# Pinned means, later constants and a GpSimd split at the hand-over from projection to attention

## The chip, the cores and the metric

The kernel runs on one core of a Trainium2 chip. The metric is the device time of one execution in microseconds. A core has five engines with a queue of instructions each: TensorE (PE; its weight loads are listed as PEld), VectorE (DVE), ScalarE (ACT), GpSimd (POOL) and SyncE (SP, which here only issues transfers). Each engine works through its own queue in order; an instruction that has to wait holds up everything behind it on that engine. POOL and SP both issue the transfers of the paged cache.

## The reference, cut to what matters

One decoder layer is computed for a prompt of 1024 tokens and for a sample group of 8 sequences with 8 new tokens each, whose 4096 past tokens lie in a paged cache (256 pages of 128 tokens). Both groups share the weights.

```python
h = rms_norm(x, norm1) * (1 + scale1) + shift1
z = h @ w_in
q, kc, vc, ks, vs, kw, vw, gates, conv..., pool_in = split(z)
q  = rms_norm(q, q_gain)                     # per head of 64 channels
ks = rms_norm(ks, k_gain[1]); kw = rms_norm(kw, k_gain[2])
k_cmp = rms_norm(compress(kc of past and new), k_gain[0]); v_cmp = compress(vc ...)
o_cmp, p_cmp = attention(q, k_cmp, v_cmp)    # compressed blocks
top_i = top_k(block importance from p_cmp)   # selected blocks
o_slc = attention(q, selected blocks of ks, vs)
o_win = attention(q, last 512 of kw, vw)
o = g0 * o_cmp + g1 * o_slc + g2 * o_win     # sigmoid gates
x = x + gate1 * (concat[o, conv(z), pool(z)] @ w_out)
x = x + gate2 * swiglu(rms_norm(x, norm2) * (1 + scale2) + shift2)
```

Every large product is done in three matmuls of a high and a low half (`hi*hi + lo*hi + hi*lo`), so each fp32 operand is first split: ACT writes the rounded high half, and DVE or POOL subtracts it from the value to get the low half (`split`, whose low half is L171 and whose high half is L175).

## The kernel before, in words

The 1088 tokens (1024 of the prompt, 64 of the samples) lie along the free axis in three chunks of 384, 384 and 320. The stages are: the conditioning and the norm; the input projection; attention for prompt and samples together; the output projection; the feed-forward part. PSUM is dealt out anew between stages (`psum_phase`): during the projection six banks hold accumulators, during attention six hold scores and two hold accumulations.

**Input projection.** Sixteen weight tiles of 128 output columns are each multiplied with the three chunks. `project` (L708) issues 24 matmuls for a chunk (eight slices of the contraction, three products each). The last four tiles are the query's, q0 to q3. For these, and for ks and kw, a coroutine `head_norm` (L752) is spawned per chunk: Square on ACT (L757), a matmul with the matrix `mean_h` on PE which forms the mean over each head's channels, the square root on ACT (L762), the reciprocal on DVE (L765), and the scaling on DVE (L766). The scaling reads the chunk's accumulator, and so sets that PSUM bank free.

**The hand-over.** `attention` (L1458) writes the masks (POOL and DVE), splits two stacks of keys (`key_stacks`, L1042: K[0] for the selected and compressed branches, K[1] for the window; each 1024 columns from the projection and 64 compressed ones), splits the first query columns (`query_parts`, L1064), writes constants that only the samples need (`constants3`, L282), and copies the sample queries and keys (`sample_setup`, L1220). The last two are issued after the last scaling of the projection (`issue_after`).

**Attention.** 32 prompt units (`prompt_attention`) alternate between branch slc and branch win: score matmuls into six PSUM banks, an evacuation on DVE with mask and minimum (L1123), exponent on ACT (L1135), two small operations by the gate on DVE (L1137 to L1141), a multiply on POOL (L1145), transposes on PE (L143) and value matmuls. Between them run the samples. Their cache is compressed in octets: eight pages of 128 KB are loaded into one of three `stream` buffers, six by SP and two by POOL (L520 to L538), and PE multiplies them in 16 matmuls, each of which is two records of the trace. The first three of the eight sequences are compressed before the hand-over. `sample_select` (L1236) then chooses blocks for a pair of sequences, after loading that pair's compressed keys (`kvc`, L1247); it runs four times. `sample_attention` reads the pages again in units of 16 (`unit`).

**What sets the order.** Stages are Python generators. A planner (`run`, L85) keeps an estimated clock for each engine. Of the tasks whose due time has come it steps the one of lowest priority number; `use` adds an estimated cost to an engine and `hold` waits for a condition. This gives the order in which instructions are written; a scheduler behind it then orders each engine's queue by its own simulation, bounded by `high_priority` and `issue_after`.

Of the kernel before, what the change touches and what calls it, by code (L numbers as in the profile page):

```python
# [17 lines left out]
P = 128  # L18
# [26 lines left out]
PACE = 0.5  # L45
EPS = 1e-6
# [16 lines left out]
class Kernel:  # L63
# [218 lines left out]
    def constants3(self, c):  # L282
        nc = self.nc
        with self.pool("ctmp") as tp:

            ti = tp.tile([P, 1], I32, name="ti")
            nc.gpsimd.iota(ti, pattern=[[0, 1]], base=0, channel_multiplier=1)
            t7 = tp.tile([P, 1], I32, name="t7")
            nc.vector.tensor_scalar(t7, ti, 7, None, op0=OP.bitwise_and)
            tv = tp.tile([P, 1], F32, name="tv")  # L290
            nc.vector.tensor_copy(tv, t7)


            di = tp.tile([P, P], I32, name="di")
            nc.gpsimd.iota(di, pattern=[[1, P]], base=P, channel_multiplier=-1)
            d7 = tp.tile([P, P], I32, name="d7")
            nc.vector.tensor_scalar(d7, di, 7, None, op0=OP.bitwise_and)
            eq = tp.tile([P, P], F32, name="eq")
            nc.vector.tensor_scalar(eq, d7, 0.0, None, op0=OP.is_equal)
            self.rsum = c.tile([P, P], F32, name="rsum")  # L300
            nc.gpsimd.memset(self.rsum, 0.0)
            for q in range(4):
                s = slice(32 * q, 32 * q + 32)
                nc.vector.tensor_copy(self.rsum[s, s], eq[s, s])


            a = tp.tile([P, 4, 64], F32, name="a")
            for b2 in range(2):
                nc.gpsimd.iota(a[64 * b2:64 * b2 + 64], pattern=[[-16, 4], [1, 64]], base=-8 * b2,
                               channel_multiplier=0, allow_small_or_imprecise_dtypes=True)  # L310
            ge = tp.tile([P, 4, 64], F32, name="ge")
            nc.vector.tensor_scalar(ge, a, 0.0, None, op0=OP.is_ge)
            ok = tp.tile([P, 4, 64], F32, name="ok")
            nc.vector.scalar_tensor_tensor(ok, a, tv[:, 0:1], ge, op0=OP.is_le, op1=OP.mult)
            self.m_new = c.tile([P, 4, 64], F32, name="m_new")
            nc.vector.tensor_scalar(self.m_new, ok, -1.0, 1e30, op0=OP.add, op1=OP.mult)


            w = tp.tile([P, 8], F32, name="w")
            nc.gpsimd.iota(w, pattern=[[1, 8]], base=0, channel_multiplier=0, allow_small_or_imprecise_dtypes=True)  # L320
            self.m_win = c.tile([P, 512], BF16, name="m_win")
            nc.gpsimd.memset(self.m_win, 0.0)
            nc.vector.tensor_scalar(self.m_win[:, 0:8], w, tv[:, 0:1], NEG, op0=OP.is_le, op1=OP.mult)


            self.sel = c.tile([P, 4, P], F32, name="sel")
            si = tp.tile([P, 4, 2, 8, 8], F32, name="si")
            for p in range(4):
                nc.gpsimd.iota(si[:, p], pattern=[[-8, 2], [0, 8], [-1, 8]], base=-64 - 16 * p,
                               channel_multiplier=1, allow_small_or_imprecise_dtypes=True)  # L330
            nc.vector.tensor_scalar(self.sel.rearrange("a p r -> a (p r)"), si.rearrange("a p b g t -> a (p b g t)"),
                                    0.0, None, op0=OP.is_equal)


            hi = tp.tile([P, 8], F32, name="hi")
            for b2 in range(2):
                nc.gpsimd.iota(hi[64 * b2:64 * b2 + 64], pattern=[[-8, 8]], base=0, channel_multiplier=1,
# [2037 lines left out]
```

## Time and profile before

| | us |
|---|---|
| median of three runs | 1656.8 (1656.56 to 1657.72) |
| the profiled execution's own time | 1654.03 |
| its span | 1652.4 |
| PE busy | 1565.2 (95%) |
| DVE busy | 1092.2 (66%) |
| ACT busy | 775.7 (47%) |
| POOL busy | 656.3 (40%) |
| mean granted clock of PE | 0.981 |

The span is what the profiler's records cover. The projection ends at about 368 us of it, attention lies between 368 and 817, and the output projection and the feed-forward part follow. A row of a timeline gives the start, the duration, the engine, the line, the operation with its tiles, and how many instructions were taken together; a bracket gives the idle time of the engine ahead of it and the instruction that ended it. The granted clock is the share of full speed at which PE was let run.

### The profile page before, as it was taken

The page shows a single profiled execution, that of the slowest core. Times are in us where ns is not written, and L with a number is a line of the kernel's source. Part 1 is how long each engine was busy: PE and PEld are TensorE (multiplying, and loading weights), DVE is VectorE, ACT ScalarE, POOL GpSimd, SP SyncE. Part 2 cuts the span into 40 slices and gives each one's busy share as a digit, 9 for nine tenths or more (in the row PEclk, how much of TensorE's full clock was granted, in tenths as well). Part 3 has the DMA queues.
Part 4 walks back from the last instruction along what each step waited for, and adds up shares of the span by engine and source line. Part 5 has one row for each costly group of instructions (what it writes and reads, how often), then busy time and mean ns, then how long its engine had stood idle before and what let it go on. Part 6 is the DMA issues. An engine that isn't in the chain of part 4 may idle for free.

```text
span 1652.4 us, 35479 instructions
## 1 busy us (share of the span) xinstructions
PE 1565.2 (95%) x12569; PEld 1388.2 (84%) x12569; DVE 1092.2 (66%) x2645; ACT 775.7 (47%) x1828; POOL 656.3 (40%) x789
## 2 busy tenths in 40 slices
PE   6999999997999899899999989999999999899998
PEld 2899997895777666566699989999999999899998
DVE  4713224876555666767589878777777775577668
ACT  3522215434765667656576534343434333344444
POOL 3111110213333133222213356554544554788765
PEclk9999999998999899999999999999999999999999
DMA  9576665425467373244696565336443335967643
GB/s 339 188 266 188 193 182 169 147 77 163 136 179 219 108 211 97 78 132 126 194 319 213 189 224 185 139 137 232 147 146 138 138 136 199 380 244 249 217 159 125
DMA packets 194659, 302.12 MB, mean 183 GB/s; under 512 B 25841, under 2 KB 131634, under 8 KB 194162
## 3 DMA queue, kind: packets, MB, share of 16 engines
q1 hardware_dynamic: 175346, 272.17, 49.5%
q0 software_dynamic: 6208, 17.38, 3.3%
q10 hardware_dynamic: 12928, 10.29, 2.1%
q8 instruction: 100, 1.64, 0.4%
q14 instruction: 77, 0.63, 0.1%
HBM read 233.43 MB, written 70.53 MB: 184 GB/s over the span
## 4 chain that ended last, share of the span: by engine, by line
PE 74%; DVE 11%; ACT 5%; DMA 4%; issue 3%; POOL 2%; SPq 0%; ACTq 0%; DVEq 0%; POOLq 0%
PE bank L139 70%; PE bank L143 4%; DVE P L1123 2%; ACT P L1135 2%; DVE w_lo L171 1%; DMA w_raw<-in_wup 1%; DMA w_raw<-in_wout 1%; ACT w_hi L175 1%; DMA x<-x_d 1%; POOL P L1145 1%; POOL b_t L171 1%; DMA x<-in_xT 1%; DVE h_lo L474 1%; DVE b_lo L171 0%; DVE ml L171 0%
## 5 line engine op out<-in xcount | busy, mean ns | idle before, releaser
L139 PE MATMUL bank<-b_hi,w_hi 128*128 128x272 f32 x1232 | 351.3, 290 | 7.0 <-DVE pair L1722 2.9
L139 PE MATMUL bank<-b_lo,w_hi 128*128 128x272 f32 x1232 | 353.5, 289 | 1.7 <-DVE b_lo L171 1.7
L139 PE MATMUL bank<-b_hi,w_lo 128*128 128x272 f32 x1232 | 348.8, 288 | 1.3 <-DVE w_lo L171 0.9
L139 PEld LDWEIGHTS bank<-b_hi,w_hi 128*128 128x128 f32 x1232 | 230.5, 189 | 10.4 <-ACT b_hi L175 4.0
L139 PEld LDWEIGHTS bank<-b_lo,w_hi 128*128 128x128 f32 x1232 | 232.4, 189 | 2.4 <-DVE b_lo L171 2.3
L139 PEld LDWEIGHTS bank<-b_hi,w_lo 128*128 128x128 f32 x1232 | 230.6, 189 | 1.8 <-DVE w_lo L171 1.1
L1145 POOL TENSOR_SCALAR P<-P,st 128x128 f32<-128x128 f32 (+10 forms) x192 | 109.1, 582 | 232.7 <-DVE st L1141 141.3
L171 DVE TENSOR_TENSOR w_lo<-w_raw,w_hi 128x512 fp32r<-128x512 f32 (+2 forms) x120 | 114.6, 965 | 81.8 <-ACT w_hi L175 81.6
L171 POOL TENSOR_TENSOR w_s<-w_raw 128x512 f32<-128x512 f32 (+1 forms) x88 | 124.3, 1412 | 70.3 <-DVE w_lo L171 53.4
L175 ACT ACTIVATE w_hi<-w_raw 128x512 fp32r<-128x512 f32 (+2 forms) x122 | 80.6, 677 | 132.5 <-PE bank L139 87.7
L139 PEld LDWEIGHTS bank<-stream 128*128 128x128 f32 x1056 | 128.8, 200 | 16.0 <-issue 11.9
L139 PE MATMUL bank<-stream 128*128 128x128 f32 x1056 | 135.1, 286 | 1.8 <-DMA stream<-in_cacheA 1.1
L1135 ACT ACTIVATE P<-P,st 128x128 f32<-128x128 f32 (+12 forms) x192 | 112.7, 588 | 45.8 <-DVE st L1129 28.6
L171 POOL TENSOR_TENSOR x<-x,d_m 128x272 f32<-128x272 f32 x136 | 118.0, 887 | 34.2 <-DVE x L1925 17.5
L139 PE MATMUL bank<-h_hi,w_hi 128*128 128x384 f32 (+1 forms) x384 | 129.4, 337 | 0.4 <-DVE q L766 0.4
L139 PE MATMUL bank<-h_hi,w_lo 128*128 128x384 f32 (+1 forms) x384 | 126.6, 330 | 0.0
L139 PE MATMUL bank<-h_lo,w_hi 128*128 128x384 f32 (+1 forms) x384 | 126.4, 329 | 0.0
L171 DVE TENSOR_TENSOR w_lo<-w_s,w_hi 128x512 fp32r<-128x512 f32 (+1 forms) x124 | 115.7, 935 | 15.9 <-ACT w_hi L175 13.7
L139 PE MATMUL bank<-g,w_hi 128*128 128x272 f32 x616 | 121.4, 293 | 4.7 <-DVE x L1925 4.7
L139 PE MATMUL bank<-g,d_hi 128*128 128x272 f32 x616 | 119.1, 289 | 2.3 <-DVE x L1928 1.6
L1925 DVE SCALAR_TENSOR_TENSOR x<-bank,mod,x 128x272 f32<-128x272 f32 (+1 forms) x200 | 90.2, 476 | 39.1 <-PE bank L139 28.2
L175 ACT ACTIVATE w_hi<-w_s 128x512 fp32r<-128x512 f32 (+1 forms) x124 | 76.6, 621 | 64.5 <-PE bank L139 35.4
(376 smaller groups left out, 3756.3 us busy)
## 6 DMA issues: line engine op xcount, KB each, us to landing
g<-g_d SPq DMA_DIRECT2D x63, 544.0 KB, 6.1
g_d<-f_s SPq DMA_DIRECT2D x57, 544.0 KB, 3.4
wada<-in_wada SPq DMA_DIRECT2D x96, 256.0 KB, 5.3
stream<-in_cacheA SPq DMA_DIRECT2D x192, 128.0 KB, 3.2
w_raw<-in_wup SPq DMA_DIRECT2D x40, 512.0 KB, 4.3
unit<-in_cacheB SPq DMA_DIRECT2D x152, 128.0 KB, 2.4
stream<-in_cacheB SPq DMA_DIRECT2D x104, 128.0 KB, 2.2
w_raw<-in_wout SPq DMA_DIRECT2D x24, 512.0 KB, 5.7
```

Source lines behind the costliest of these rows:

```text
L139: return self.nc.tensor.matmul(out, lhsT, rhs, start=start, stop=stop, skip_group_check=chain)
L143: return self.nc.tensor.transpose(out, in_, self.ident if ident is None else ident)
L171: (self.nc.vector if eng == "dve" else self.nc.gpsimd).tensor_tensor(out, a, b, op=op)
L175: self.last_hi = self.nc.scalar.activation(hi, src, AF.Copy)
L474: nc.vector.scalar_tensor_tensor(lk, t, sh[:, k, 0:1], hk.bitcast(F32), op0=OP.add, op1=OP.subtract)
L1123: nc.vector.tensor_tensor_reduce(out=Pt[:, 2 * g + hl, col:col + n], in0=S[g][:, p0:p0 + n], in1=mk, scale=-1.0, scalar=3e38, op0=OP.add, ...
L1135: nc.scalar.activation(Ps, Ps, AF.Exp, scale=-1.0, bias=sy[:, g, 0:1], accum_out=sy[:, g, 1:2])
L1145: nc.gpsimd.tensor_scalar(Ps, Ps, sy[:, g, 3:4], 0.0, op0=OP.mult, op1=OP.add)
L1925: self.last_gate = nc.vector.scalar_tensor_tensor(out[:, :n], acc[:, :n], self.mod[:, 5, m, 0:1], out[:, :n], op0=OP.mult, op1=OP.add)
```

## The change

The change has four parts.

1. The last query tile, q3, is `PINNED`: of each chunk only four of the eight contraction slices are written, then the planner steps other tasks until the preceding `head_norm` has written its instructions, and the other four slices are issued after that head's mean matmul.
2. In `attention`, `query_parts` comes ahead of `key_stacks`. `constants3` leaves its place ahead of `sample_setup` and is issued after the last softmax evacuation of the first prompt unit. Its scratch tiles now live in the pool of the attention stage, not in a pool of their own. The samples' attention is held until the constants are written.
3. In `key_stacks`, the low halves of the second stack (window) are computed on GpSimd.
4. `sample_select` for a pair is held until the selection of the pair before is over (`selected`).

```diff
+PINNED = ("q3",)
...
     def constants3(self, c):
         nc = self.nc
-        with self.pool("ctmp") as tp:
-
-            ti = tp.tile([P, 1], I32, name="ti")
...
+        tp = c
+
+
+        ti = tp.tile([P, 1], I32, name="ti")
...
-    def project(self, w, h, ch, n):
-        acc = self.bank()
-        for k in range(KT):
+    def project(self, w, h, ch, n, acc=None, ks=range(KT)):
+        acc = self.bank() if acc is None else acc
+        for k in ks:
             self.mm3(acc[:, :n], (w[0][:, k], w[1][:, k]), (h[ch][0][:, k, :n], h[ch][1][:, k, :n]),
                      k == 0, k == KT - 1)
         return acc[:, :n]
...
-            self.mm(m[:, :n], self.mean_h, sq[:, :n], True, True)
+            self.last_mean = self.mm(m[:, :n], self.mean_h, sq[:, :n], True, True)
...
-                        acc = self.project(w, h, ch, n)
+                        if nm in PINNED:
+                            heads = self.heads
+                            acc = self.project(w, h, ch, n, None, range(KT // 2))
+                            yield from self.hold(lambda: self.heads > heads)
+                            with self.tc.issue_after(self.last_mean.ins):
+                                self.project(w, h, ch, n, acc, range(KT // 2, KT))
+                        else:
+                            acc = self.project(w, h, ch, n)
                         step(nm, ch, acc, c0, n)
...
         for j in range(2):
             kh, kl = self.K[j]
             for a, n, src in ((64, SEQ, self.ksw[:, j, 0:SEQ]), (0, 64, self.kcp)):
-                self.split(kh[:, a:a + n], kl[:, a:a + n], src, n)
+                self.stacks_at = self.split(kh[:, a:a + n], kl[:, a:a + n], src, n, eng="pool" if j else "dve")
                 yield max(self.t["dve"], self.t["act"]) - 1.0
-        self.stacks_at = max(self.t["dve"], self.t["act"])
...
+            if u == 0 and hl == 1:
+                self.first_evac = self.last_evac
+                self.scored = True
             yield 0.0
...
-        yield from self.hold(lambda: self.cmp_done >= 2 * p + 2)
+        yield from self.hold(lambda: self.cmp_done >= 2 * p + 2 and self.selected == p)
...
+        self.selected += 1
...
     def attention(self, ap, kp_, opened):
         self.masks(ap)
         self.use("dve", 1.0)
+        self.query_parts(ap, 0)
         yield from self.key_stacks()
-        self.query_parts(ap, 0)
         with self.tc.issue_after(self.last_scale.ins):
-            self.constants3(ap)
             self.sample_setup(ap)
-        self.use("dve", 5.0)
         kp_.__exit__(None, None, None)
         pp = opened.enter_context(self.pool("prompt"))
         self.spawn(lambda: 1.8 + self.v_done / 32, self.prompt_attention(pp))
+        yield from self.hold(lambda: self.scored)
+        with self.tc.issue_after(self.first_evac.ins):
+            self.constants3(ap)
+        self.use("dve", 3.2)
+        self.constants_done = True
 
     def sample(self, opened, cp, batches):
         share = lambda: 1.9 + 0.4 * (self.cmp_done - EARLY) / (NB - EARLY)
         self.spawn(share, self.compress(cp, batches, 0))
         sp = opened.enter_context(self.pool("samp", "left"))
+        yield from self.hold(lambda: self.constants_done)
         yield self.t["dve"]
```

How this moves the instructions is seen in the engines' queues. First PE, at the end of the input projection, before; `h_hi_107` and `h_lo_108` are the halves of the third chunk, `h_sq,mean_h` is a head's mean (128x384 of the second chunk, 128x320 of the third):

```order
L139 MATMUL bank<-h_hi_107,w_hi 128x320
L139 MATMUL bank<-h_lo_108,w_hi 128x320
L139 MATMUL bank<-h_hi_107,w_lo 128x320
L139 MATMUL bank<-h_sq,mean_h 128x384
L139 MATMUL bank<-h_sq,mean_h 128x320
L139 MATMUL bank<-stream 128x128 x16
```

And the same place now; the line numbers of the changed file are higher by one here:

```order
L140 MATMUL bank<-h_hi_107,w_hi 128x320
L140 MATMUL bank<-h_lo_108,w_hi 128x320
L140 MATMUL bank<-h_hi_107,w_lo 128x320
L140 MATMUL bank<-h_sq,mean_h 128x384
L140 MATMUL bank<-h_hi_107,w_hi 128x320
L140 MATMUL bank<-h_lo_108,w_hi 128x320
L140 MATMUL bank<-h_hi_107,w_lo 128x320
```

The second chunk's mean stood behind all 24 matmuls of the third chunk; now it stands behind twelve of them, and the other twelve follow it. The third chunk's mean (128x320) is still the last matmul ahead of the octet. PE executes the same matmuls, only the order is another.

Second, DVE at the hand-over, before; `kl_3450` is the low half of the first key stack and `kl_3452` that of the second, `ql` the query's, and L264 to L273 write the masks:

```order
L171 TENSOR_TENSOR kl_3450<-kv__98,kh_3449 128x1024
L171 TENSOR_TENSOR kl_3450<-kcp,kh_3449 128x64
L264 CAST m_slc<-m 128x128
L264 CAST m_edge<-m 128x128
L264 CAST m_cmp<-m 128x8
L171 TENSOR_TENSOR kl_3452<-kv__98,kh_3451 128x1024
L171 TENSOR_TENSOR kl_3452<-kcp,kh_3451 128x64
L273 COPY m_edge<-m_slc 128x128
L171 TENSOR_TENSOR ql<-q,qh 128x512 x2
L765 RECIPROCAL h_sq<-h_sq 128x384
L765 RECIPROCAL h_sq<-h_sq 128x320
L766 SCALAR_TENSOR_TENSOR q<-bank,qgain_s,h_sq 128x384
```

And now:

```order
L767 RECIPROCAL h_sq<-h_sq 128x384
L172 TENSOR_TENSOR ql<-q,qh 128x512
L768 SCALAR_TENSOR_TENSOR q<-bank,qgain_s,h_sq 128x384
L172 TENSOR_TENSOR kl_3450<-kv__98,kh_3449 128x1024
L265 CAST m_slc<-m 128x128
L172 TENSOR_TENSOR kl_3450<-kcp,kh_3449 128x64
L265 CAST m_edge<-m 128x128
L265 CAST m_cmp<-m 128x8
L172 TENSOR_TENSOR ql<-q,qh 128x512
L274 COPY m_edge<-m_slc 128x128
L767 RECIPROCAL h_sq<-h_sq 128x320
L768 SCALAR_TENSOR_TENSOR q<-bank,qgain_s,h_sq 128x320
```

The second chunk's reciprocal and scaling moved ahead of the first stack's low half, and the second stack's low half is gone from DVE. Behind these rows stood, before, the last scaling, the operations of `constants3` mixed with those of `sample_setup` and the first selection's memsets, and then the first evacuation; now only the setup and the memsets stand there. On POOL the two subtractions of `kl_3452` stand behind the last `iota` of the constants and ahead of the two cache pages (`stream`) that POOL issues.

Third, SP's queue where it comes to the second selection's compressed keys (`kvc`); `stream` are pages of octets. Before:

```order
L530 ISA
L530 DMA stream<-in_cacheA 128x256
L1247 DMA kvc<-cmp_d 128x512
L526 TENSOR_LOAD pt
L530 ISA
L530 DMA stream<-in_cacheA 128x256
```

And now:

```order
L532 ISA
L532 DMA stream<-in_cacheA 128x256
L1258 DMA kvc<-cmp_d 128x512 x2
L528 TENSOR_LOAD pt
L532 ISA
L532 DMA stream<-in_cacheA 128x256
```

From the hand-over on SP's queue held, before, the first selection's two `kvc` loads, 6 stream loads (one octet), 16 unit loads, 18 stream loads, one `kvc` load, 10 stream loads and the other `kvc` load. Now it holds the first two `kvc` loads, 18 stream loads (three octets), the same 16 unit loads, 30 stream loads, and then two `kvc` loads together: the unit loads stand behind two more octets, and the second selection's loads behind 48 stream loads where the first of them stood behind 24.

More of the change, by code (lines that the diff above doesn't have):

```diff
@@ L283, in constants3 @@
         nc = self.nc
-        with self.pool("ctmp") as tp:
-            ti = tp.tile([P, 1], I32, name="ti")
[L287 to L337, printed above, removed]
-                               allow_small_or_imprecise_dtypes=True)
-            hg = tp.tile([P, 8], F32, name="hg")
-            nc.vector.tensor_scalar(hg, hi, 0.0, None, op0=OP.is_ge)
-            self.hind = c.tile([P, 8], F32, name="hind")
-            nc.vector.scalar_tensor_tensor(self.hind, hi, 7.0, hg, op0=OP.is_le, op1=OP.mult)
@@ new lines, in constants3 @@
+        nc.vector.tensor_scalar(d7, di, 7, None, op0=OP.bitwise_and)
+        eq = tp.tile([P, P], F32, name="eq")
+        nc.vector.tensor_scalar(eq, d7, 0.0, None, op0=OP.is_equal)
+        self.rsum = c.tile([P, P], F32, name="rsum")
+        nc.gpsimd.memset(self.rsum, 0.0)
+        for q in range(4):
+            s = slice(32 * q, 32 * q + 32)
+            nc.vector.tensor_copy(self.rsum[s, s], eq[s, s])
+        a = tp.tile([P, 4, 64], F32, name="a")
+        for b2 in range(2):
+            nc.gpsimd.iota(a[64 * b2:64 * b2 + 64], pattern=[[-16, 4], [1, 64]], base=-8 * b2,
+                           channel_multiplier=0, allow_small_or_imprecise_dtypes=True)
@@ new lines, in constants3 @@
+        self.m_win = c.tile([P, 512], BF16, name="m_win")
+        nc.gpsimd.memset(self.m_win, 0.0)
+        nc.vector.tensor_scalar(self.m_win[:, 0:8], w, tv[:, 0:1], NEG, op0=OP.is_le, op1=OP.mult)
+        self.sel = c.tile([P, 4, P], F32, name="sel")
+        si = tp.tile([P, 4, 2, 8, 8], F32, name="si")
+        for p in range(4):
+            nc.gpsimd.iota(si[:, p], pattern=[[-8, 2], [0, 8], [-1, 8]], base=-64 - 16 * p,
+                           channel_multiplier=1, allow_small_or_imprecise_dtypes=True)
@@ new lines, in constants3 @@
+        nc.vector.tensor_scalar(self.sel.rearrange("a p r -> a (p r)"), si.rearrange("a p b g t -> a (p b g t)"),
+                                0.0, None, op0=OP.is_equal)
+        hi = tp.tile([P, 8], F32, name="hi")
+        for b2 in range(2):
+            nc.gpsimd.iota(hi[64 * b2:64 * b2 + 64], pattern=[[-8, 8]], base=0, channel_multiplier=1,
+                           allow_small_or_imprecise_dtypes=True)
+        hg = tp.tile([P, 8], F32, name="hg")
+        nc.vector.tensor_scalar(hg, hi, 0.0, None, op0=OP.is_ge)
@@ L2186, in build @@
         self.combined = 0
+        self.scored = self.constants_done = False
         self.n2_done = 0
@@ L2221, in build @@
         self.post_free = True
+        self.selected = 0
         self.constants2()
```

20 lines of the change are left out of this document (19 added, 1 removed).

## The prediction

> **What bounds the kernel now.** I read the page first, then TensorE's waits, the row of every engine around its longest wait, and last the same stretches as windows. The page's first part:
>
> ```profile
> PE 1565.2 (95%) x12569; PEld 1388.2 (84%) x12569; DVE 1092.2 (66%) x2645; ACT 775.7 (47%) x1828; POOL 656.3 (40%) x789
> ```
>
> PE is busy for 95% of the span, so another engine matters only where it makes PE stop. The waits of PE from 378 to 800 us (us in all, times, the longest):
>
> ```profile
> PE bank L143 <- POOL P L1145: 12.1, 6, 3.2
> PE bank L139 <- DVE q L766: 6.6, 1, 6.6
> PE bank L139 <- DVE st L1123: 5.0, 5, 2.7
> PE bank L139 <- DMA stream<-in_cacheA: 1.1, 1, 1.1
> ```
>
> One wait of 6.6 us stands alone: the hand-over from the input projection to attention. PE's rows there (start, duration, then what it does; in brackets the idle time before it and its releaser):
>
> ```profile
> 363.33 0.32 PE L139 MATMUL bank<-h_hi,w_hi 128*128 128x320 f32 x1
> ...
> 366.86 1.50 PE L139 MATMUL bank<-h_sq,mean_h 128*128 128x384 f32 x4
> 368.19 3.73 PE L139 MATMUL bank<-stream 128*128 128x128 f32 x32
> 378.50 0.89 PE L139 MATMUL bank<-kh,qh 64*128 64x192 f32 x2 [6.58 <-DVE q L766]
> ...
> 380.06 0.36 PE L139 MATMUL bank<-kh,qh 64*128 64x128 f32 x1
> 383.18 0.44 PE L139 MATMUL bank<-kh,qh 64*128 64x128 f32 x1 [2.71 <-DVE st L1123]
> ...
> 384.61 8.53 PE L139 MATMUL bank<-stream 128*128 128x128 f32 x64
> 393.07 1.00 PE L143 MATMUL bank<-ident,P 64*128 64x64 f32 x12
> ```
>
> The last means end the projection, one octet of the cache (x32) fills PE to 371.92, then PE stands for 6.58 us until the heads' scaling on DVE, computes the first scores, and stands 2.71 us more for the softmax evacuation (L1123): 9.3 us idle. DVE has no gap there:
>
> ```profile
> 363.97 2.56 DVE L765 RECIPROCAL h_sq<-h_sq 128x384 f32<-128x384 f32 x1 [2.81 <-ACT h_sq L762]
> ...
> 368.47 1.23 DVE L171 TENSOR_TENSOR kl<-kv__98,kh 128x1024 fp32r<-128x1024 f32 x1 [1.30 <-ACT kh L175]
> ...
> 370.86 1.16 DVE L171 TENSOR_TENSOR kl<-kv__98,kh 128x1024 fp32r<-128x1024 f32 x1
> ...
> 372.17 1.28 DVE L171 TENSOR_TENSOR ql<-q,qh 128x512 fp32r<-128x512 f32 x2
> 373.37 4.55 DVE L765 RECIPROCAL h_sq<-h_sq 128x384 f32<-128x384 f32 x2
> 377.85 0.97 DVE L766 SCALAR_TENSOR_TENSOR q<-bank,qgain_s,h_sq 128x384 f32<-128x384 f32 x2
> 378.74 0.14 DVE L289 TENSOR_SCALAR t<-ti 128x1 int32<-128x1 int32 x1
> ...
> 379.67 0.48 DVE L1223 MEMSET qb<- 128x512 f32 x1
> ...
> 380.55 0.57 DVE L1226 COPY qb<-q 64x256 f32<-64x256 f32 x2
> ...
> 382.65 0.28 DVE L1123 CUSTOM_DVE_ANT_0 P<-bank,m_slc 128x128 f32<-128x128 f32 x1
> ```
>
> In order: both stacks' low halves (kl), the query's (ql), two reciprocals (2.56, the second 4.55 - 2.56 = 2.0), two scalings, then 3.9 us of constants and sample setup before the first evacuation at 382.65. The first scores sit behind both scalings, since these empty the PSUM banks that the scores take. The windows (us; busy time of PE, PEld, DVE, ACT, POOL; granted clock; DMA share; GB/s):
>
> ```profile
> 371.90:378.50 6.60, 0.03 (x1) 0.03 (x1) 6.60 (x9) 0.00 (x0) 3.75 (x14) 0.87 0.67 200
> 384.60:387.00 2.40, 2.40 (x12) 2.39 (x12) 1.12 (x10) 2.40 (x17) 0.56 (x2) 0.50 0.64 201
> 387.00:393.00 6.00, 6.00 (x55) 5.95 (x54) 1.69 (x8) 1.62 (x9) 4.45 (x13) 1.00 0.36 103
> 392.00:396.00 4.00, 4.00 (x38) 2.93 (x38) 2.08 (x13) 2.72 (x11) 1.08 (x2) 1.00 0.92 282
> 414.40:421.00 6.60, 6.51 (x34) 5.48 (x35) 3.09 (x26) 4.73 (x22) 2.95 (x8) 0.50 0.00 0
> 817.00:1652.40 835.40, 807.23 (x6321) 798.50 (x6321) 631.08 (x1141) 374.59 (x840) 458.22 (x444) 0.99 0.57 197
> ```
>
> The idle time has a second price: until 387.0 the granted clock is 0.50, and an octet's matmul then takes 2.40/12 = 0.20 us, against 3.73/32 = 0.117 in the first octet. Each us of octets at half clock thus loses 1 - 0.117/0.20 = 0.41 us. From 817 on PE is busy for 807.23 of 835.40 us in an order that the change keeps, so what is gained before stays.
>
> **The change part by part.**
>
> *Pinned means.* No matmul is added. The mean of q3's second chunk stood behind the 24 matmuls of the third; now it follows the twelfth. These 24 take 366.86 - 363.33 = 3.53 us, 0.147 each, so the mean starts 1.8 us earlier, at 365.1, and ends (half of 1.50) at 365.85. ACT's square roots are
>
> ```profile
> 370.62 0.98 ACT L762 ACTIVATE h_sq<-bank,eps 128x384 f32<-128x384 f32 x2
> 383.01 1.28 ACT L1135 ACT_TABLE_LOAD   x1 [11.41 <-issue]
> ```
>
> 0.49 each, and this one no longer stands behind the splits: done at 366.4. DVE then has reciprocal 2.56 (369.0), one ql 0.64, scaling 0.49: 370.2, before the octet ends. The third chunk's mean stays last.
>
> *Low halves and query parts.* The first stack's kl (1.23) still precedes the scores: 371.4, so they start about when the octet ends, at 371.92, and the 6.58 us wait goes. Its short piece and the casts take the rest of the 370.86 - 368.47 = 2.39 us between the two kl rows: 372.6; the second ql 0.64: 373.2. The second stack's kl (372.17 - 370.86 = 1.3 with its short piece) leaves DVE. **Late next** is the third chunk's scaling: reciprocal 2.0, scaling 0.49: 375.7. The window scores need its bank.
>
> *Constants.* Of the 3.9 us from 378.74 to 382.65, the setup from 379.67 to 381.12 (380.55 + 0.57) stays, without the five constants' operations between its own some 1.4 us; 2.5 us leave the path. The displaced constants run between later evacuations, under PE's octets (DVE is busy for 1.69 of 387.0 to 393.0); uncovered, they would cost that 2.5. The evacuation starts at 375.7 + 1.4 = 377.1. The table load (1.28), which stood at 383.01 although ACT had been idle for 11.41 us, moves ahead of it; nothing in the sum counts on that.
>
> *The planner's holds and due times* (`selected`, `constants_done`, `stacks_at`, 3.2 for 5.0) issue nothing; they act through the order alone, which is the first and the third rival.
>
> *GpSimd.* The page's group for the same kind of operation, and POOL's rows:
>
> ```profile
> L171 POOL TENSOR_TENSOR w_s<-w_raw 128x512 f32<-128x512 f32 (+1 forms) x88 | 124.3, 1412 | 70.3 <-DVE w_lo L171 53.4
> 370.81 1.24 POOL L279 TENSOR_SCALAR_AFFINE_SELECT rowok<-rowok 128x1 f32<-128x1 f32 x1
> ...
> 374.42 0.33 POOL L337 IOTA hi<- 64x8 f32 x2
> 375.80 1.17 POOL L530 DMA_DIRECT2D stream<-in_cacheA  x2 [1.06 <-issue]
> 386.44 3.88 POOL L1145 TENSOR_SCALAR P<-P,st 128x128 f32<-128x128 f32 x12 [9.46 <-ACT P L1135]
> ```
>
> 1.41 us for 512 columns is 2.8 for 1024 (an estimate); behind the iotas (374.75) it ends near 377.6. Only the window scores' second matmuls want it, and these stand behind the evacuation's first half us, so it is hidden, with nothing to spare: each us that POOL starts later would be PE's. Two things are queued behind it: two octet pages, whose issue slips from 375.80 to 378.9 (allow 0.3 us, bounds 0 and 0.9), and the multiplies by st, which start far later and end 2.7 us (393.07 - 386.44 - 3.88) before the transposes take them. DVE may suffer too: rowok, one column wide, took 1.24 us just while DVE's two-input kl ran (370.86 to 372.02). Turned round, kl on POOL may hold DVE's setup copies until it ends: bounds 0 and 1.4 us. The Trainium skill, page "SBUF — State Buffer", section "SBUF: two separate sides", speaks against this part of the change: VectorE and GpSimd share one port pair as an exclusive lock, and the loser waits out a whole instruction. The rowok row agrees; by this rule the sum below would lie at its upper end, 1.4 us later.
>
> *The sum.* The following octet started 384.61 - 382.65 = 1.96 us behind the first evacuation. It would now start at 379.1, or 380.5 with the whole lock: 5.5 or 4.1 us earlier; I take the middle, 4.8. Against that: the clock that stayed at 0.50 for 2.4 us of octets will, with the octets reached sooner after an idle stretch, perhaps stay for 3.4: 0.4 us. It could be 0 (a gain of 2.4 x 0.41 = 1.0) or 5 us (a loss of 1.1). The pages cost 0.3. Net 4.8 - 0.4 - 0.3 = 4.1 us; ends 5.5 + 1.0 = 6.5 and 4.1 - 1.1 - 0.9 = 2.1. The profiled execution took 1654.03 us (span 1652.4), 2.8 below the runs' median of 1656.8; the saving is the same in both: 1649.9 on the profiled one, **1652.7 us** on the median. The Trainium skill, page "TensorE: Matmul & The Clock Gate", section "Part 1: The HAM clock gate", has the clock follow a window of some 3.4 us, so that gaps of 2.5 us would not halve it. By it the sum would take the 1.0 gain; 414.40 to 421.00, at 0.50 with PE busy for 6.51 of 6.60 us, disagrees at least on how soon it returns.
>
> **Rivals.**
>
> *The order behind wins more.* The change also moves the octets and the paged loads (`selected == p` holds the second selection back until the first is over):
>
> ```profile
> 416.31 6.12 PE L139 MATMUL bank<-stream 128*128 128x128 f32 x32
> 422.46 1.37 SPq L530 DMA_DIRECT2D stream<-in_cacheA  x3
> ```
>
> This octet runs at half clock behind short waits, SP's next page can only start when it has freed its buffer, at 422.46, and from 414.40 to 421.00 nothing is transferred. With octets closer together one could lie among those short waits. Worth: 6.5 x 0.41 = 2.7 of clock and some 1.0 of waits just ahead of it (an estimate: the POOL P row of the waits gives 12.1 in 6, and half of one such is taken), on top of 4.1: 7.8, so 1649.0. Against it: waits of that length can form elsewhere in the new order.
>
> *The clock eats it.* Both octets at half clock throughout: 64 x 0.20 = 12.8 in place of 8.53, 4.3 lost of 4.8, 0.3 for the pages: gain 0.2, 1656.6. For it speaks the clock at 387.0, which came back only 8.5 us after PE did; against it, that the gaps shrink.
>
> *Slower: octets starve.* Octets now stand closer together, and 16 unit loads have been moved behind those of two more octets:
>
> ```profile
> 375.51 9.82 SPq L530 DMA_DIRECT2D unit<-in_cacheB  x16
> 475.06 1.58 PE L139 MATMUL bank<-stream 128*128 128x128 f32 x12 [1.14 <-DMA stream<-in_cacheA]
> ```
>
> An octet is 1 MB: 3.7 us at the 282 GB/s of 392 to 396, exactly the 3.73 that PE spends on it. Back to back, nothing is spare. From the point where three octets stand with less than 3.7 us of other work between, each waits; at the 475.06 row's 1.1 us for nine of them, +9.9 - 4.1: 1662.6. Against it: that wait occurred once in 440 us.
>
> *It doesn't do what it says* would be the mean still waiting in ACT's queue; the Square of the third chunk cannot start before the chunk ends, so the square root precedes it. I give this nothing of its own.
>
> **How the numbers follow.** Forecast 0.50 (own range 1650.3 to 1654.7), order 0.16 (1649.0), clock 0.16 (1656.6), starving 0.18 (1662.6). A measurement here tells 0.2%, 3.3 us, from no change. The forecast's 4.1 is beyond that in three quarters of its range: 0.37 faster, 0.13 same. So faster 0.37 + 0.16 = 0.53, same 0.13 + 0.16 = 0.29, slower 0.18. The range reaches from below the order's case, 1646, into the starving one, 1661 (its milder half); about 0.05 and 0.1 stay outside.
>
> **What would show it.** Right: no wait for q at L766 near 372; a wait of about 2.5 us for the third chunk's scaling or the evacuation; the octet pair at 379 to 380 instead of 384.61; kl on POOL at 2.5 to 2.8 us. The lock: DVE copies of over 1 us beside it. Clock: the octet pair longer than 9 us. Starving: PE waits for stream in the list of waits, over 3 us in all. The forecast falls if PE reaches 817's work less than 3 us or more than 7 us earlier than before.

## The result, and the profile after

The changed kernel takes 1673.3 us (median of six runs, 1668.49 to 1679.92) against 1657.2 us before (also the median of six): the ratio is 1.0101, with a 95% interval of 1.0072 to 1.013. The forecast was 1652.7 us, faster, with a range to 1661. The sign was wrong, and the time lies outside the range.

The profiled execution took 1668.49 us, with a span of 1666.9. PE's rows at the hand-over, in the changed kernel (start, duration, what; in brackets the idle time before and its releaser):

```profile
359.85 0.31 PE L140 MATMUL bank<-h_hi,w_hi 128*128 128x320 f32 x1
...
364.70 0.81 PE L140 MATMUL bank<-h_sq,mean_h 128*128 128x320 f32 x2 [0.53 <-ACT h_sq L759]
365.34 3.73 PE L140 MATMUL bank<-stream 128*128 128x128 f32 x32
369.01 0.36 PE L140 MATMUL bank<-kh,qh 64*128 64x192 f32 x2
...
371.96 0.33 PE L140 MATMUL bank<-kh,qh 64*128 64x128 f32 x1 [2.04 <-DVE q L768]
373.87 0.44 PE L140 MATMUL bank<-kh,qh 64*128 64x128 f32 x1 [1.58 <-DVE st L1131]
...
375.31 9.33 PE L140 MATMUL bank<-stream 128*128 128x128 f32 x64
```

The hand-over did what it was meant to do. The first scores follow the octet at once, the wait of 6.58 us is gone, and what is late next are the third chunk's scaling (2.04) and the evacuation (1.58). From the start of the single octet to that of the pair of octets it took 384.61 - 368.19 = 16.42 us before and 375.31 - 365.34 = 9.97 us now. (The single octet itself starts between 364.3 and 368.9 from one execution to the next, also in versions that are equal up to there, so the distance is what can be compared.) One small cost lies ahead of the octet, where this distance does not see it. The third chunk's mean now waits 0.53 us for its Square on ACT, where the second chunk's mean used to fill that time; from the third chunk's first matmul to the octet it takes 365.34 - 359.85 = 5.49 us, where it took 368.19 - 363.33 = 4.86 us: 0.63 us more.

What was gained is more than lost again behind it. The rows below are windows of both kernels, first before, then after: from the pair of octets to the first output matmul, and after it also from there to the end (us; busy time of PE, PEld, DVE, ACT, POOL; granted clock; DMA share; GB/s).

```profile
384.61:816.90 432.29, 399.87 (x3976) 282.46 (x3976) 269.13 (x1152) 273.78 (x756) 130.69 (x231) 0.96 0.48 145
```

```profile
375.31:830.83 455.52, 405.35 (x3976) 284.74 (x3975) 275.26 (x1175) 278.53 (x761) 132.64 (x235) 0.95 0.48 143
830.83:1666.90 836.07, 808.96 (x6321) 801.92 (x6321) 625.37 (x1132) 372.14 (x828) 456.32 (x440) 0.99 0.56 196
```

The last stage is as it was (836.07 us against 835.40 from 817 on). The rest of attention, with the same 3976 matmul records, takes 455.52 - 432.29 = 23.2 us longer: PE is idle for 50.2 us in place of 32.4, and busy for 5.5 us more with the same records, at a mean granted clock of 0.95 in place of 0.96. Counted by the columns that PE's matmuls stream, 7.5 of the 23.2 us lie in the first quarter of this stretch (136.7 us against 129.2) and 11.3 in its last tenth (53.7 against 42.4). PE's longest waits in these two windows (three dots stand for rows left out), before:

```profile
PE bank L143 <- POOL P L1145: 12.1, 6, 3.2
PE bank L143 <- DVE st L1123: 2.5, 4, 1.5
...
PE bank L139 <- DMA unit<-in_cacheB: 2.2, 2, 1.6
...
PE bank L139 <- DMA stream<-in_cacheA: 1.1, 1, 1.1
PE bank L139 <- ACT mh L175: 1.1, 1, 1.1
PE bank L139 <- ACT pair L622: 0.9, 1, 0.9
```

And after:

```profile
PE bank L144 <- POOL P L1153: 11.3, 6, 3.6
PE bank L140 <- ACT pair L624: 8.1, 4, 5.3
PE bank L140 <- DMA unit<-in_swinKV: 6.3, 1, 6.3
PE bank L144 <- ACT e L1399: 4.2, 4, 1.6
PE bank L140 <- ACT w_hi L176: 4.1, 1, 4.1
...
PE bank L140 <- ACT spt L162: 2.6, 1, 2.6
PE bank L140 <- DVE pair L589: 2.3, 1, 2.3
```

None of the new waits is near the hand-over, and none is of an instruction that the change edits. PE waits for the compression's second half (`pair`: 8.1 + 2.3 in place of 0.9), for the first pair's window unit (`swinKV`, 6.3), for the exponents and transposes of the last units (`e`, `spt`), and for the high halves of the first output weights (`w_hi`, 4.1). Everything here is executed by the same code as before, in another order.

### The profile page after: what moved, and what is told of

Its sections match the earlier page's. It is cut to its first block, busy times and chain, and to the rows that moved or that the text cites. A ratio compares the mean times of both kernels' runs of the same rounds, so it can differ in the third digit from the quotient of the medians.

```text
span 1666.9 us, 35454 instructions
## 1 busy us (share of the span) xinstructions
PE 1568.7 (94%) x12569; PEld 1390.2 (83%) x12569; DVE 1089.8 (65%) x2641; ACT 779.4 (47%) x1829; POOL 657.6 (39%) x791
## 4 chain that ended last, share of the span: by engine, by line
PE 41%; DVE 7%; issue 4%; DMA 3%; POOL 2%; ACT 2%; ACTq 0%; DVEq 0%; POOLq 0%; SPq 0%
PE bank L140 40%; PE bank L144 1%; DVE w_lo L172 1%; DVE P L1131 1%; DMA w_raw<-in_wup 1%; DMA w_raw<-in_wout 1%; POOL w_s L172 1%; DMA x<-x_d 1%; ACT w_hi L176 1%; ACT P L1143 1%; POOL b_t L172 0%; DVE b_lo L172 0%; DVE x L1941 0%; POOL f_T L172 0%; DVE f_s L172 0%
## 5 line engine op out<-in xcount | busy, mean ns | idle before, releaser
L1153 POOL TENSOR_SCALAR P<-P,st 128x640 f32<-128x640 f32 (+11 forms) x192 | 108.1, 577 | 232.7 <-DVE st L1149 158.3
L1143 ACT ACTIVATE P<-P,st 128x640 f32<-128x640 f32 (+10 forms) x192 | 112.8, 589 | 47.8 <-DVE st L1131 22.9
L1768 POOL TENSOR_TENSOR pair<-pair,f_v 128x272 f32<-128x272 f32 x44 | 44.0, 1000 | 152.0 <-DVE f_v L1738 123.4
```

What stands on the lines that cost most here:

```text
L1143: nc.scalar.activation(Ps, Ps, AF.Exp, scale=-1.0, bias=sy[:, g, 0:1], accum_out=sy[:, g, 1:2])
L1153: nc.gpsimd.tensor_scalar(Ps, Ps, sy[:, g, 3:4], 0.0, op0=OP.mult, op1=OP.add)
L1768: nc.gpsimd.tensor_tensor(g[:, 1], s1, v, op=OP.mult)
```

## The experiments

Theory A: the time is lost to the order which the planner writes for the rest of attention, because the change alters the planner's account (which engine is booked, when a task may start). Theory B: it is lost to what was moved at the hand-over itself (GpSimd's split, the page loads queued behind it, the constants). The measures used for all of them are the distance from the first octet to the pair of octets (H), the distance from there to the first output matmul (R), and the median time of the runs. The kernel before was run again beside each group of runs, with medians of 1653.3 to 1657.2 us, and the ratio is to those, so between groups the ratios are compared. H and R are of one execution each. The changed kernel and run 8, with the same matmul order from the pair on, differ by 3.3 us in R, so a difference of that size in R shows nothing by itself.

| kernel | H | R | median us | ratio to before (95%) |
|---|---|---|---|---|
| before | 16.42 | 432.3 | 1657.2 | |
| changed | 9.97 | 455.5 | 1673.3 | 1.0101 (1.0072 to 1.013) |
| 1 changed, old account | 9.97 | 436.0 | 1651.5 | 0.9982 (0.9964 to 1.0) |
| 2 changed, split on DVE | 11.06 | 436.8 | 1653.4 | 0.9986 (0.9973 to 0.9999) |
| 3 before, split on GpSimd | 17.30 | 443.1 | 1666.4 | 1.0082 (1.0061 to 1.0102) |
| 4 the same, old account | 17.31 | 435.8 | 1660.2 | 1.0041 (1.0026 to 1.0055) |
| 5 as 1, last unit in a unit buffer | 9.98 | 430.2 | 1646.7 | 0.9947 (0.9926 to 0.9968) |
| 6 changed, last unit in a unit buffer | 9.96 | 449.9 | 1664.0 | 1.0046 (1.0031 to 1.0061) |
| 7 changed, last pair early | 9.97 | 447.9 | 1663.0 | 1.0049 (1.0027 to 1.0072) |
| 8 changed, not pinned | 12.15 | 458.9 | 1676.5 | 1.0104 (1.008 to 1.0129) |
| 9 changed, constants booked with 7.0 | 9.97 | 465.8 | 1677.1 | 1.0133 (1.01 to 1.0166) |
| 10 changed, selections not held | 9.97 | 458.7 | 1674.8 | 1.0117 (1.0083 to 1.0152) |
| 11 before, constants booked with 3.2 | 16.43 | 441.4 | 1665.5 | 1.006 (1.0041 to 1.0079) |
| 12 as 5, constants booked with 2.0 | 10.54 | 450.1 | 1663.9 | 1.0047 (1.0028 to 1.0065) |

**1 and 2: the account or the split.** In the first run GpSimd still does the second stack's low halves, but the planner's clocks are set as if DVE did them:

```diff
+                plan = dict(self.t)
-                self.stacks_at = self.split(kh[:, a:a + n], kl[:, a:a + n], src, n, eng="pool" if j else "dve")
+                self.split(kh[:, a:a + n], kl[:, a:a + n], src, n, eng="pool" if j else "dve")
+                if j:
+                    self.t.update(plan)
+                    self.use("dve", 0.07 + n * 0.00105, self.use("act", 0.09 + n * 0.00084))
                 yield max(self.t["dve"], self.t["act"]) - 1.0
+        self.stacks_at = max(self.t["dve"], self.t["act"])
```

> The changed kernel in every instruction of the hand-over (low halves of the second stack on GpSimd too), but the planner books those low halves on DVE as before, so that it writes the rest of attention in another order: the last pair of sequences begins its units after 84.0% of the stage's matmul columns, where the changed kernel has 92.7% and the kernel before 89.5%. Theory A (the new order of attention loses the time): the pair of octets starts near 375 us as in the changed kernel, and the whole is faster than the changed kernel by over 8 us, 1650 to 1662 where before is 1657. Theory B (GpSimd's split and what is queued behind it loses it): within 4 us of the changed kernel, 1669 to 1677.

The second run takes the changed kernel and leaves `key_stacks` as it was before the change, with both stacks on DVE.

> The changed kernel with the second stack's low halves back on DVE. Its matmul order is the same as that of the run above (84.0%). Theory A: within 4 us of that run, the hand-over some 1.3 us longer. Theory B: faster than that run by over 8 us, 1650 to 1660.

Theory A held. The first run takes 1651.5 us, 0.9982 of the kernel before where the changed kernel takes 1.0101, which is some 20 us less, at the same H of 9.97; the second takes 1653.4. The two have the same order of matmuls in attention, and differ by 1.1 us in H: that is what GpSimd's split is worth. In the changed kernel it cost DVE nearly nothing, because it ran beside a reciprocal. POOL and DVE there:

```profile
370.23 2.34 POOL L172 TENSOR_TENSOR kl<-kv__98,kh 128x1024 fp32r<-128x1024 f32 x1
```

```profile
369.18 2.14 DVE L767 RECIPROCAL h_sq<-h_sq 128x320 f32<-128x320 f32 x1
371.36 0.55 DVE L768 SCALAR_TENSOR_TENSOR q<-bank,qgain_s,h_sq 128x320 f32<-128x320 f32 x1
371.96 0.48 DVE L1234 MEMSET qb<- 128x512 f32 x1
372.36 0.30 DVE L1241 COPY kn<-kv__98 128x128 f32<-128x128 f32 x1
...
373.34 0.29 DVE L1131 CUSTOM_DVE_ANT_0 P<-bank,m_slc 128x128 f32<-128x128 f32 x1
```

The split took 2.34 us (2.8 was estimated), and only `kn` was touched (0.30 us; it took 0.15 before). The setup from 371.96 to the evacuation at 373.34 took 1.38 us (1.4 was estimated).

**3 and 4: the split alone on the kernel before.** In the third run `key_stacks` is the changed one and nothing else; in the fourth the planner books it on DVE, as in the first run.

> The kernel before with the second stack's low halves on GpSimd, nothing else. The planner books them on GpSimd, and the last pair begins at 92.7%, as in the changed kernel; octets and first selection stay as before (2.4%, 8.2%). Theory A: slower than before by 5 to 15 us, the loss lying in the second half of attention. Theory B: slower by about 10 us too, but at the hand-over and in the first octets.

> The kernel before with the second stack's low halves on GpSimd, booked on DVE: the matmul order is that of the kernel before (89.5%). Theory A: the same as before within 3 us, or 1 to 2 us faster, since DVE has 1.3 us less ahead of the reciprocals. Theory B: slower by about 10 us, as the run above.

The third run is slower by 0.82%. R grows by 10.8 us (443.1 against 432.3), of which 8.2 lie in the second half of the columns, where theory A had put them. The fourth has the matmul order of the kernel before but for a few places, and is slower by 0.41%, more than the 3 us that theory A allowed and less than theory B's 10; its R is 3.5 us above that of the kernel before. So each theory has a part here: 443.1 - 435.8 = 7.3 us of the third run's R go with the order, and what the fourth run loses (4.5 us by the medians, 6.8 by the ratio) goes with the split itself. Of that, 2.3 us are visible at the hand-over, and where the others lie is not shown. POOL and DVE of the fourth run:

```profile
371.69 2.82 POOL L171 TENSOR_TENSOR kl<-kv__98,kh 128x1024 fp32r<-128x1024 f32 x1
```

```profile
371.63 3.42 DVE L171 TENSOR_TENSOR ql<-q,qh 128x512 fp32r<-128x512 f32 x2
```

Here the split falls on DVE's two `ql`, which read two SBUF tiles each: 3.42 us in place of the 1.28 quoted of the kernel before, that is 2.1 us lost to win the 1.3 of the moved kl, and H is 0.9 us longer. This is the lock that the prediction bounded with 1.4 us, at another place. The Trainium skill, page "SBUF — State Buffer", section "SBUF: two separate sides", states it for a DVE operation with two SBUF inputs against a GpSimd operation that reads SBUF; these rows agree, and the changed kernel's rows agree too, since a reciprocal has one input. The other 1.4 us are the pair of octets (9.95 us in place of 8.53, at a mean granted clock of 0.73 in place of 0.86).

**5 and 6: the output weights.** The changed kernel and the first run have one new wait in common, for `w_hi` at the end. In both, the last unit of the samples lies in a `stream` buffer, where in the kernel before it lay in a `unit` buffer. The thought was that the first load of the output weights then waits for the matmuls that read that buffer. Which kind the last unit gets follows from the moment at which the three stream buffers join the rotation. The fifth run (on the first) lets them join one load later, the sixth (on the changed kernel, with `> 2`) two loads later:

```diff
-        if self.cmp_done == NB and self.stream_left:
+        self.joins += self.cmp_done == NB
+        if self.joins > 1 and self.stream_left:
```

> The run with the old account (1651.5), in the same matmul order from the first scores to the last unit; the three stream buffers only join the samples' unit buffers one load later, so that the last unit (the last pair's window) lies in a unit buffer, as in the kernel before, and not in a stream buffer, whose place the first output weights need. Theory A (the first output weights wait for the last unit's buffer): their load starts 8 us or more ahead of the first output matmul, the 5.5 us wait for w_hi falls below 2, and the whole is 3 to 6 us faster, 1646 to 1649. Rival (the last unit's own softmax chain sets the end, and w_hi only came last): the wait changes its name, the time stays within 2 us of 1651.5.

> The changed kernel with the stream buffers joining two loads later: the last unit in a unit buffer, the last pair still beginning at 92.7% of the stage's matmul columns. Theory A: 3 to 6 us faster than the changed kernel (1673), 1667 to 1670, the rest of its loss remaining. Rival: within 2 us of it.

The fifth run has exactly the matmul order of the first in attention. The last matmul of the samples and the first output matmul, and SP's first load of the output weights, in the first run:

```profile
806.84 1.97 PE L140 MATMUL bank<-stream,spt 128*64 128x128 f32 x16 [2.73 <-ACT spt L162]
814.34 1.04 PE L140 MATMUL bank<-mh,w_hi 128*128 128x272 f32 x3 [5.52 <-ACT w_hi L176]
```

```profile
808.86 11.27 SPq L1542 DMA_DIRECT2D w_raw<-in_wout  x6
```

And in the fifth:

```profile
807.47 1.09 PE L140 MATMUL bank<-unit,spt 128*64 128x128 f32 x16 [2.73 <-ACT spt L162]
808.49 0.77 PE L140 MATMUL bank<-mh,w_hi 128*128 128x272 f32 x4
```

```profile
799.15 24.73 SPq L1544 DMA_DIRECT2D w_raw<-in_wout  x10
```

In the first run the load starts as the last unit's matmuls end (808.86 and 806.84 + 1.97). In the fifth it starts 9.7 us earlier, the 5.52 us wait is gone, and R falls from 436.0 to 430.2: theory A. This is the fastest version: 1646.7 us, 0.53% under the kernel before.

In the changed kernel the wait has the same name but not the same reason. SP's first load, ACT's rows and the last unit's matmuls there:

```profile
820.68 17.46 SPq L1537 DMA_DIRECT2D w_raw<-in_wout  x6
```

```profile
828.06 0.75 ACT L176 ACTIVATE mh<-pair 128x272 fp32r<-128x272 f32 x2 [3.37 <-DMA pair<-mix_d]
828.72 0.26 ACT L162 ACTIVATE part<-bank 128x128 f32<-128x128 f32 x1
828.87 1.39 ACT L176 ACTIVATE mh<-pair 128x272 fp32r<-128x272 f32 x4
830.17 0.61 ACT L176 ACTIVATE w_hi<-w_raw 128x512 fp32r<-128x512 f32 x1
```

```profile
824.75 1.98 PE L140 MATMUL bank<-stream,spt 128*64 128x128 f32 x16 [2.56 <-ACT spt L162]
```

The first load starts 4 us ahead of the last unit's matmuls, so it did not wait for them, and these loads land within 5.8 us. But in ACT's queue the split of the weights stands behind splits of mixed results (`mh`), for which ACT waits 3.37 us until their transfer through `mix_d` lands. What PE waits for there is this place in ACT's queue.

The sixth run gains 5.6 us of R and 0.55% of the whole, some 9 us, more than theory A's 3 to 6. Two waits are gone: that for `w_hi` (4.11 us; ACT's first split of the weights now comes at 822.90, ahead of the last unit's `spt` and of the later `mh`) and the one for the window unit (6.29 us in the changed kernel, 0.63 here). In the changed kernel the window unit's load had been issued right behind 18 stream loads, and took 8.3 us to land, where the others of its kind take from 5.1. The matmul order changed as well, so the gain cannot be put down to the last unit's buffer.

**7: the last pair.** In the changed kernel the last pair of sequences begins late. With `> 3` in the line above the planner begins it early.

> The changed kernel with the stream buffers joining three loads later; the planner then begins the last pair at 80.5% of the columns, and the last unit is in a unit buffer. If the late last pair costs the changed kernel its time: at least 6 us faster than the run above, 1655 to 1662, the last tenth of the stage taking no longer than in the kernel before (42 us). If the loss lies in the first half of attention (waits for the compression's pair and for the first window unit): within 4 us of the run above, with the last tenth shorter all the same.

The whole stays the same, 1663.0 against 1664.0, but that does not clear the late pair. The last tenth of the columns takes 46.5 us, where it takes 53.0 in the sixth run, 53.7 in the changed kernel and 42.4 before; the new order takes 4.5 us more ahead of it. And the seventh run has a wait for `w_hi` again, though its last unit lies in a `unit` buffer and its first load had started at 795.88:

```profile
825.96 2.18 PE L140 MATMUL bank<-mh,w_hi 128*128 128x272 f32 x8 [5.43 <-ACT w_hi L176]
```

There too ACT's split stands behind an `mh` (824.63) that had waited for `mix_d`. So a late last pair goes with a longer last tenth, and what the early pair wins there, the order that comes with it loses elsewhere; whether the late pair alone costs the time is not shown.

**8: the pinning alone.** The changed kernel without the halves of q3; its matmul order in attention is that of the changed kernel.

> The changed kernel without the pinned halves; its matmul order from the first scores on is the same. The second chunk's mean stands behind all 24 matmuls of the third chunk again. If the pinning sets the hand-over, all of DVE's chain is 1.8 us later: from the start of the first octet to that of the pair of octets 11.8 us in place of 9.97, and the whole 1 to 3 us slower than the changed kernel. If something else hides it: 10.0 and no difference.

H grows by 2.18 us (1.8 had been worked out). Less the 0.63 us that the pinning costs ahead of the octet, it gains 1.55 us. In the whole this cannot be seen: 1.0104 and 1.0101 of the kernel before are the same within their intervals.

**9 and 10: other draws.** The ninth run books the constants with 7.0 us on DVE (`self.use("dve", 7.0)` for 3.2); the tenth takes `and self.selected == p` out.

> The changed kernel with one number of the planner changed: the constants are booked on DVE with 7.0 us where it has 3.2; what is executed at the hand-over is the same. The matmul order differs from the changed kernel's only in the first half of attention (the compression stands further from its own evacuations); the last pair still begins at 92.7% of the columns, and the last unit lies in a unit buffer. Theory A (the loss is the order that the planner happens to write, through waits for the compression's pair, the first window unit and the output weights): PE's waits for pair fall from 10.4 us to under 4, the whole is 8 to 18 us faster than the changed kernel, 1655 to 1665. Rival (the loss belongs to what was moved at the hand-over): within 4 us of the changed kernel, 1669 to 1677.

> The changed kernel without the hold on the selections (selected). In the kernel before the same hold leaves the order as it is; here the planner writes another: the second selection at 6.5% of the columns instead of 10.2%, the last pair at 84.2% instead of 92.7%. If the hold is what makes the order bad: 1645 to 1656, as with the old account. If each new order is simply another draw: anywhere from 1647 to 1673, and no wait that the hold explains is gone; the last unit is in a stream buffer still, so the output weights come late by some 5 us either way.

Neither is faster. The ninth, 1677.1, is near what the rival had written (1669 to 1677) and far from theory A's 1655 to 1665, and the tenth lies 2 us above the whole span of its draws. PE's waits in the ninth, over the same stretch:

```profile
PE bank L144 <- POOL P L1153: 13.6, 5, 4.4
PE bank L144 <- ACT e L1399: 6.0, 5, 1.9
PE bank L140 <- DMA stream<-in_cacheA: 5.8, 2, 3.8
PE bank L140 <- ACT pair L624: 5.1, 2, 4.2
```

Those for `pair` did fall, to 5.1 us from 10.4, and the last unit did lie in a unit buffer, but others came: for P, for e, and for octet pages, and PE is busy for 418.99 us in R, 13.6 more than in the changed kernel, at a mean granted clock of 0.93 in place of 0.95. So the waits for `pair` are a part of one draw, not the cause. The rival's reason is ruled out by the first run, which executes the same hand-over and is not slower than before. The selection's hold is not the cause either: without it the time is the same, with other waits (w_hi 7.4 us, pair 10.1).

**11 and 12: one number, no instruction.** If the order is a draw, it must be possible to spoil the kernel before, and the fastest version, by the booked cost alone. The eleventh run has `self.use("dve", 3.2)` for 5.0 in the kernel before, which is the number that the change writes; the twelfth has 2.0 for 3.2 in the fifth.

> The kernel before with one number of the planner changed, the constants booked on DVE with 3.2 us (the changed kernel's number) where it has 5.0. Nothing is moved at the hand-over by hand; the planner writes another order for the rest (last pair at 84.2% of the columns, the last unit in a stream buffer). Theory A (the loss comes from whichever order the planner writes): hand-over as in the kernel before (16.4 us from the first octet to the pair of octets), yet the whole differs from before by more than 4 us, slower rather than faster, since the output weights come late by some 5 us: 1660 to 1675. Rival (the order after the hand-over matters little, and the loss of the changed kernel belongs to its parts): within 3 us of before.

> The fastest version so far (old account, last unit in a unit buffer, 1646.7) with the constants booked with 2.0 us where it has 3.2. The planner then writes nearly the changed kernel's order (last pair at 92.7%, last unit in a stream buffer again), while the hand-over executes the same. Theory A: the gain at the hand-over stays (10.0 us from the first octet to the pair of octets), and the whole is slower than 1646.7 by 10 to 28 us, 1657 to 1675. Rival: within 4 us of 1646.7.

Both times came as theory A has it. The eleventh keeps H (16.43), and loses 9.1 us in R: 0.6% slower. Its reason did not come: the output weights are not late, and PE waits only 1.79 us, for `mh`, ahead of the first output matmul. The waits that grow most are those for `pair` (7.7 us in all, in place of 0.9). The twelfth stays near its H (10.54, with 0.50 us for an octet page), loses 19.9 us in R, and is 17 us slower. Its window, against the fifth run's; first the twelfth, then the fifth:

```profile
379.15:829.23 450.08, 406.20 (x3975) 286.28 (x3975) 272.44 (x1168) 279.53 (x760) 132.98 (x235) 0.94 0.48 145
```

```profile
378.34:808.49 430.15, 398.75 (x3976) 281.77 (x3975) 268.79 (x1165) 278.79 (x758) 133.04 (x235) 0.96 0.51 150
```

Of these 19.9 us, 7.45 are PE busy for longer with the same work, at a mean granted clock of 0.94 in place of 0.96, and 12.48 are idle.

What stays open is which property makes an order good. R lay between 430 and 466 us over the fourteen kernels. One single cause is shown in an unchanged order of matmuls: the output weights' buffer of run 1, 5.8 us of R. Two more are seen where the order changed as well: the window unit's load (5.7 us less of its wait in the sixth run) and the late last pair (6.5 us in the last tenth). The rest is spread over waits that change with every draw. No run gives the changed hand-over the order of the kernel before; run 1 has an order of its own.

## Why the prediction was wrong

- **The pinned means** were right in kind: 1.8 us worked out, 2.18 measured in H in run 8. "The third chunk's mean stays last" was taken to cost nothing; it costs 0.63 us ahead of the octet, so 1.55 are left.
- **The first scores behind the octet, and the third chunk's scaling late next** were right. The scores start at 369.01, when the octet ends, and the next wait is 2.04 us for that scaling; about 2.5 was written.
- **Constants and setup** were right: 1.4 us worked out, 1.38 measured; the displaced constants ran between later evacuations.
- **GpSimd's split** was right in kind and a little too dear: 2.34 us in place of 2.8, hidden, pages issued at 372.79, 2.5 us ahead of the pair of octets, with no wait for them. The lock hardly struck at the place where it was looked for (0.15 us on `kn`): DVE was in a reciprocal for most of that time; run 4 shows it at 2.1 us where DVE was in a two-input subtraction.
- **The sum of the hand-over** was undersized: H fell by 6.45 us, where 5.5 to 4.1 was written and 4.8 taken; the pair of octets took 9.33 us in place of 8.53, 0.8 lost to the clock where 0.4 was taken. With the 0.63 ahead of the octet the net is 6.45 - 0.8 - 0.63 = 5.0, against 4.4 without the pages' 0.3, and inside the bounds of 2.1 to 6.5. Run 1, with the same hand-over and the old account, takes 1651.5 us, near the 1652.7 forecast; but its order is a new one too, and its R is 3.7 us longer than before, so that this closeness is in part luck.
- **The step that failed** is the one on the planner's holds and due times: they "issue nothing; they act through the order alone", and the sum gave that order zero. It measured some 20 us between kernels that execute the same hand-over (R of 455.5 and 436.0; 1.0101 and 0.9982 of the kernel before). The first output matmul came at 830.83 us where it had come at 816.90, and the prediction had said that it falls if this is not 3 to 7 us earlier. The argument that what is gained before 817 stays was made for the last stage, where it held (836.07 against 835.40), and was silently used for the 432 us between the hand-over and 817, which the planner had written anew. Moving the split to GpSimd alone rebooks 1.3 us of DVE, and in run 3 R grew by 10.8 us, 7.3 of them more than in run 4, which has nearly the order of before.
- **The rivals.** "The order behind wins more" and "octets starve" both put a price on the order, but each on one mechanism, read from one place, with ends of -3.7 and +9.9 us. The starving did not happen: PE waited for octet pages once in the changed kernel, for 0.5 us. The slower case was priced at 1662.6, 11 us short, and the chance of slower at 0.18. "The clock eats it" was 0.8 us on the pair of octets, and 5.5 us over all of R, of which the prediction priced the first 9 us only.

## What to carry to other kernels

Where a planner or scheduler orders the work by booked costs, an edit changes two things, what is executed and what is booked; time them apart, by giving the edited kernel the old account, before the edit is judged. The order behind an edit is a term of the sum: its size can be gauged by changing one booked number and nothing else, and here that moved the whole by 9 and 17 us where the edit itself won 6 at the hand-over. A buffer that the last unit of one stage happens to be given can hold back the first load of the next; the wait that shows it is on the split of that load, and the cure is in the rotation of the buffers. But read the load's own start and the queue of the splitting engine before you believe the name of the wait: here the same wait had two reasons. And where one run shifts the loss from one part of a stage to another, time the parts, not only the whole.

## What the runs showed of the hardware

The stretches at half clock last 3.4 us or a multiple of it. Windows of the kernel before, ahead of, in and behind one such stretch:

```profile
393.80:397.20 3.40, 3.40 (x27) 2.06 (x26) 2.52 (x19) 2.88 (x12) 0.86 (x3) 1.00 0.76 241
397.20:400.60 3.40, 3.40 (x24) 2.72 (x21) 3.17 (x24) 3.09 (x16) 2.55 (x8) 0.50 0.42 125
400.60:404.00 3.40, 3.40 (x30) 2.94 (x29) 0.17 (x1) 0.41 (x2) 0.29 (x2) 0.99 0.00 0
```

The middle window is wholly at half clock with PE shown busy throughout, and the window from 414.40 to 421.00 in the prediction (6.6 us) lies in two such steps. Now the changed kernel, from the end of its single octet into the pair of octets:

```profile
369.10:372.50 3.40, 1.15 (x13) 0.83 (x13) 3.31 (x6) 0.48 (x1) 3.25 (x7) 1.00 0.61 160
372.50:375.90 3.40, 2.03 (x14) 1.95 (x14) 3.36 (x35) 2.23 (x13) 1.47 (x4) 0.51 0.47 148
375.90:379.30 3.40, 3.40 (x17) 3.40 (x17) 3.26 (x28) 2.09 (x12) 1.00 (x3) 0.50 0.00 0
379.30:382.70 3.40, 3.40 (x33) 3.40 (x32) 0.11 (x1) 0.00 (x0) 3.40 (x11) 0.99 0.12 39
```

Two steps again. The Trainium skill, page "TensorE: Matmul & The Clock Gate", section "Part 1: The HAM clock gate", gives a window of about 3.4 us, and these rows agree in length. The prediction's conclusion from it, that gaps of 2.5 us would not halve the clock, does not hold here: the longest gap at the changed hand-over is 2.04 us, and the clock was halved behind it. What starts a step stays open, since ahead of the one at 397.20 PE is shown busy for 3.40 of 3.40 us. What was not expected is how much these steps add up: the same 3976 matmul records of attention kept PE busy for 398.75 us in the fifth run, at a mean granted clock of 0.96, and for 418.99 us in the ninth, at 0.93.
